# Low parts of the streamed weight tiles on DVE in one step of 1024 columns, instead of on POOL in four

## The chip, the cores and the metric

The kernel runs on one core of a Trainium2 chip. The metric is the device time of one execution in microseconds; lower is better. A measurement is the median of several runs. The engines are named as the profile names them: PE (matmul) with its weight loads PEld, DVE (vector), ACT (scalar), POOL (GpSimd) and SP, whose queue issues most transfers.

## The reference, cut to what matters

The model is a two-layer diffusion backbone of width 1024 over 512 latent tokens and 256 context tokens, in float32. Each layer does, in essence:

```python
h  = rms_norm(x,  pre_g[i]) * (1.0 + scale)  + shift     # 512 x 1024
hc = rms_norm(xc, pre_g[i]) * (1.0 + cscale) + cshift    # 256 x 1024
p  = t @ w_in                # for t = h and hc: q, k, v, z
y  = (attention(q, k, v) * silu(z)) @ w_out
x  = x + gate * rms_norm(y, post_g[i])
```

Layer 0 is a differential attention with 8 heads (two softmaxes per head, one subtracted from the other), with outputs for latent and context tokens. Layer 1 is a grouped-query attention with 8 query heads and 2 key/value heads, with outputs for the latent tokens alone. `w_in` has 4096 columns in layer 0 and 2560 in layer 1.

## The kernel before, in words

**Products from split operands.** To keep float32 accuracy, each operand is split into a high part (a rounded cast, `whi` for weights) and a low part (what the cast left over, `wlo`). A product is three matmuls, in `mm3` (lines 146 to 149): high by high (L147), one operand's low part by the other's high part (L148), and high by low (L149). Weights come in tiles of 128 x 1024.

**The stream of weights.** `WStream` (`ws`) keeps a list of tiles in the order in which they are needed. For each it calls `wsplit` (lines 206 to 212): SP issues the load into a `raw` tile (L208; 512 KB), ACT casts it into `whi` (L210), and the engine named in the list subtracts `whi` from `raw` to make `wlo`, in `pieces` (L204). `pieces` cuts the columns into steps of 256 where that engine is POOL, and does them in one step where it is DVE:

```python
n = w // -(-w // 256) if eng is nc.gpsimd else w
for i in range(0, w, n):
    eng.tensor_tensor(dst[:, i:i + n], a[:, i:i + n], b[:, i:i + n], op)
```

There are two `raw` buffers, so a load starts when the tile two before it has been read by both ACT and the engine of the low part. There are three or four pairs of `whi`/`wlo`; a pair comes free when PE has used it.

Of the streamed tiles, 28 are layer 0's q, k, v and z, 20 are layer 1's (of which 8 to 11 are its k and v), and 16 are the two `w_out`. The first four tiles of layer 0 go another way, in quarters, through `w_split`. Before the change the low parts of 46 of the 64 streamed tiles are made by POOL (44 that the change touches, and tiles 9 and 11 of layer 1, which `KVE` gives to it), and those of 18 by DVE (the 16 of `w_out`, and tiles 8 and 10).

**What else the engines do.** In attention, `s_units` (layer 0, from line 829) and `s1_units` (layer 1) make scores on PE; DVE takes the maximum (L850, L1384), ACT the exponential `p` (L853, L1390), DVE the reciprocal of its sum (L856, L1391), POOL scales `p` (L218), and in layer 0 DVE then adds the two softmaxes (L861). PE transposes `p` (L910, L1405), ACT and DVE split the result into `ah` (L913, L1408) and `al` (L914, L1409), and PE multiplies by the values (L154). For layer 1's queries, `q_proj` takes a projection out of PSUM with DVE (`ta` L1243, `tb` L1245), POOL adds the two (`q`, L1248) and makes the factor `qrs` (L1256, L1257); `q_tr` transposes `q` on PE (L1341) and splits it into `qh` (ACT, L1344) and `ql` (DVE, L1345). At the start of layer 1, DVE also makes the residual gate from streamed tiles `gw` (L1443, L1445).

**What sets the order.** The program is written out in the order that a planner in the kernel (`flow`, with a running clock, costs and due times) chooses; it doesn't look at the engine that makes a low part. The framework then puts the instructions of each engine in order, by priorities and by its own estimate of times. On the chip each engine works through its list in that order; an instruction that waits holds all behind it on that engine.

Of the kernel before, what the change touches and what calls it, by code (L numbers as in the profile page):

```python
# [82 lines left out]
def tile_backbone(  # L83
# [23 lines left out]
    nc = tc.nc  # L107
# [155 lines left out]
    ws = WStream()  # L263
# [3 lines left out]
    def add_wout(layer):  # L267
        for c, n in (OUTC, OUTC1)[layer]:
            per = 1024 // n
            for k in range(KT // per):  # L270
                src = w_out[layer, k * per * P:(k + 1) * per * P, c:c + n].rearrange("(k p) n -> p k n", p=P)
                ws.add(("o", layer, c, k), src, nc.vector)
# [9 lines left out]
    for kind, h in fill0:  # L282
        a_keys += {"qk": [(h, 0), (h, 1)], "v": [(h, 2), (h + 1, 2)], "z": [(h, 3)]}[kind]
    for h, i in a_keys:
        ws.add((h, i), a_w[h * 4 + i], nc.gpsimd)
    add_wout(0)
    for i in (8, 9, 10, 11):
        ws.add(i, b_w[i], (nc.vector, nc.gpsimd)[KVE[i - 8]])
    for kind, i in [("q", 0)] + fill1:
        for g in (2 * i, 2 * i + 1) if kind == "q" else (12 + i,):  # L290
            ws.add(g, b_w[g], nc.gpsimd)
    add_wout(1)

    def after(prev):
# [1359 lines left out]
```

## Time and profile before

| | us |
|---|---|
| median of three runs (826.65, 828.59, 830.71) | 828.59 |
| the profiled execution, as timed | 825.61 |
| its span in the profile | 823.8 |

The page of the profile gives each engine's busy time as a share of the span. The view by line groups equal instructions: how many, their busy time, the mean of one, and how long the engine was idle just before them and which instruction ended that. The view of waits sums that idle time by who waited for whom. The view of windows gives each engine's busy time and the granted PE clock in a stretch of time. The timeline lists instructions by start and duration, with the idle time before one and its releaser in brackets.

### The profile page before, as it was taken

The page shows a single profiled execution, that of the slowest core. Times are in us where ns is not written, and L with a number is a line of the kernel's source. Part 1 is how long each engine was busy: PE and PEld are TensorE (multiplying, and loading weights), DVE is VectorE, ACT ScalarE, POOL GpSimd, SP SyncE. Part 2 cuts the span into 40 slices and gives each one's busy share as a digit, 9 for nine tenths or more (in the row PEclk, how much of TensorE's full clock was granted, in tenths as well). Part 3 has the DMA queues.
Part 4 walks back from the last instruction along what each step waited for, and adds up shares of the span by engine and source line. Part 5 has one row for each costly group of instructions (what it writes and reads, how often), then busy time and mean ns, then how long its engine had stood idle before and what let it go on. Part 6 is the DMA issues. An engine that isn't in the chain of part 4 may idle for free. (4 is left out here: it accounts for less than half of the span.)

```text
span 823.8 us, 14331 instructions
## 1 busy us (share of the span) xinstructions
PE 792.1 (96%) x5436; PEld 699.6 (85%) x5436; DVE 483.3 (59%) x897; ACT 452.6 (55%) x985; POOL 439.3 (53%) x612
## 2 busy tenths in 40 slices
PE   7999998999999999999999999999989999999997
PEld 4688897898878898878988898898978899988986
DVE  3745566664858425765277843664676666665534
ACT  5424457565575634764467742664336665676631
POOL 1134847965476853875733212576878854643101
PEclk9999999999999999999999999999999999999999
DMA  9924201122124321414310051031641310111102
GB/s 343 355 78 141 87 29 58 63 86 78 65 103 128 115 78 65 167 34 152 122 53 26 27 205 52 13 123 52 194 140 52 103 52 2 53 52 52 47 31 102
DMA packets 35236, 77.76 MB, mean 94 GB/s; under 512 B 3424, under 2 KB 10336, under 8 KB 35168
## 3 DMA queue, kind: packets, MB, share of 16 engines
q1 hardware_dynamic: 31600, 71.71, 25.5%
q10 hardware_dynamic: 3568, 5.16, 1.8%
q8 instruction: 42, 0.69, 0.3%
q14 instruction: 26, 0.21, 0.1%
HBM read 70.56 MB, written 2.10 MB: 88 GB/s over the span
## 5 line engine op out<-in xcount | busy, mean ns | idle before, releaser
L204 POOL TENSOR_TENSOR wlo<-raw,whi 128x256 fp32r<-128x256 f32 x196 | 149.7, 795 | 104.9 <-ACT whi L210 68.6
L147 PE MATMUL bk<-whi,h 128*128 128x256 f32 (+1 forms) x592 | 177.5, 302 | 5.9 <-DVE tb L1245 2.0
L148 PE MATMUL bk<-wlo,h 128*128 128x256 f32 (+1 forms) x592 | 176.2, 299 | 0.3 <-DVE wlo L204 0.3
L149 PE MATMUL bk<-whi,h 128*128 128x256 f32 (+1 forms) x592 | 175.1, 299 | 0.1
L147 PE MATMUL bk<-h,whi 128*128 128x512 f32 (+2 forms) x416 | 147.0, 354 | 3.2 <-ACT sq L942 1.5
L149 PE MATMUL bk<-h,wlo 128*128 128x512 f32 (+2 forms) x416 | 144.9, 349 | 0.0
L148 PE MATMUL bk<-h,whi 128*128 128x512 f32 (+2 forms) x416 | 144.6, 348 | 0.0
L147 PEld LDWEIGHTS bk<-whi,h 128*128 128x128 f32 x592 | 112.9, 191 | 15.5 <-issue 3.6
L148 PEld LDWEIGHTS bk<-wlo,h 128*128 128x128 f32 x592 | 113.1, 191 | 4.0 <-DVE wlo L204 0.5
L149 PEld LDWEIGHTS bk<-whi,h 128*128 128x128 f32 x592 | 112.3, 191 | 3.9 <-DVE h L1209 0.3
L218 POOL TENSOR_SCALAR p<-p,sm 128x768 f32<-128x768 f32 (+1 forms) x80 | 68.4, 858 | 65.8 <-DVE sm L1391 30.0
L210 ACT CAST whi<-raw 128x1024 fp32r<-128x1024 f32 x64 | 67.3, 1052 | 48.3 <-PE bk L148 19.2
L147 PEld LDWEIGHTS bk<-h,whi 128*128 128x128 f32 x416 | 78.2, 188 | 17.4 <-issue 5.1
L149 PEld LDWEIGHTS bk<-h,wlo 128*128 128x128 f32 x416 | 78.1, 188 | 8.4 <-issue 1.3
L148 PEld LDWEIGHTS bk<-h,whi 128*128 128x128 f32 x416 | 78.3, 188 | 6.8 <-issue 0.3
L853 ACT ACTIVATE p<-sc,sm 128x768 f32<-128x768 f32 (+1 forms) x68 | 59.6, 879 | 30.1 <-DVE sm L850 30.0
L850 DVE TENSOR_REDUCE sm<-sc 128x1 f32<-128x768 f32 (+1 forms) x68 | 60.5, 916 | 16.5 <-PE sc L845 16.5
L204 POOL TENSOR_TENSOR sz<-sz,za 128x192 f32<-128x192 f32 (+1 forms) x48 | 32.5, 699 | 42.0 <-ACT za L184 42.0
L861 DVE SCALAR_TENSOR_TENSOR p<-p,sm,p 128x768 f32<-128x768 f32 (+1 forms) x34 | 39.0, 1146 | 24.4 <-POOL p L218 23.5
L913 ACT CAST ah<-bk 128x512 fp32r<-128x512 f32 x56 | 31.8, 589 | 30.8 <-PE bk L910 26.8
L914 DVE TENSOR_TENSOR al<-bk,ah 128x512 fp32r<-128x512 f32 x56 | 37.4, 683 | 16.9 <-ACT ah L913 16.8
L1409 DVE TENSOR_TENSOR al<-bk,ah 128x512 fp32r<-128x512 f32 x48 | 32.1, 685 | 25.6 <-ACT ah L1408 24.8
(236 smaller groups left out, 1688.4 us busy)
## 6 DMA issues: line engine op xcount, KB each, us to landing
raw<-in_a_w SPq DMA_DIRECT2D x28, 512.0 KB, 3.5
araw<-in_ada_w SPq DMA_DIRECT2D x12, 1024.0 KB, 5.2
raw<-in_b_w SPq DMA_DIRECT2D x20, 512.0 KB, 3.9
ag<-in_ada SPq DMA_DIRECT2D x16, 512.0 KB, 7.8
raw<-in_w_out SPq DMA_DIRECT2D x16, 512.0 KB, 3.5
sw<-qr ACTq DMA_DIRECT2D x32, 128.0 KB, 2.1
gw<-in_ada_w SPq DMA_DIRECT2D x8, 512.0 KB, 4.1
xnt<-in_xlT SPq DMA_DIRECT2D x4, 512.0 KB, 5.7
```

The costliest lines, as they stand in the source:

```text
L147: nc.tensor.matmul(o, ahi, bhi, start=start, stop=False)
L148: nc.tensor.matmul(o, ahi, blo, start=False, stop=False)
L149: nc.tensor.matmul(o, alo, bhi, start=False, stop=stop)
L204: eng.tensor_tensor(dst[:, i:i + n], a[:, i:i + n], b[:, i:i + n], op)
L210: nc.scalar.copy(hi, r)
L218: (nc.vector if eng == "v" else nc.gpsimd).tensor_scalar(dst, src, s_, 1.0, ALU.mult, ALU.mult)
L850: nc.vector.tensor_reduce(mx, scv, AX.XY if nk == T else AX.X, ALU.max, negate=True)
L853: nc.scalar.activation(pv_, scv, AF.Exp, bias=mx, accum_out=l[:, m:m + 1])
L861: nc.vector.scalar_tensor_tensor(ps_[0], pt, r, ps_[0], ALU.mult, ALU.add)
L913: nc.scalar.copy(ah, tr)
L914: nc.vector.tensor_tensor(al, tr, f32(ah), ALU.subtract)
L1409: nc.vector.tensor_tensor(al, tr, f32(ah), ALU.subtract)
```

## The change

The list of weight tiles names DVE instead of POOL for all of layer 0's tiles (`a_keys`) and for layer 1's q and z. So `pieces` makes one step of 128 x 1024 of each on DVE instead of four of 128 x 256 on POOL.

```diff
     for h, i in a_keys:
-        ws.add((h, i), a_w[h * 4 + i], nc.gpsimd)
+        ws.add((h, i), a_w[h * 4 + i], nc.vector)
     add_wout(0)
     for i in (8, 9, 10, 11):
         ws.add(i, b_w[i], (nc.vector, nc.gpsimd)[KVE[i - 8]])
     for kind, i in [("q", 0)] + fill1:
         for g in (2 * i, 2 * i + 1) if kind == "q" else (12 + i,):
-            ws.add(g, b_w[g], nc.gpsimd)
+            ws.add(g, b_w[g], nc.vector)
```

The order changes with it on every engine, since the framework orders by its estimates. Two places matter below. In the names, the first number tells tiles of one kind apart.

The first is POOL at the start of layer 1's attention, while the queries of heads 0 and 1 are made. Before, from the third of four sums, `q_849`, to the third weight tile:

```order
L1248 TENSOR_TENSOR q_849_6541<-ta_850_6542,tb_851_6543 128x256
L204 TENSOR_TENSOR wlo_861_6591<-raw_859_6588,whi_860_6590 128x256 x4
L204 TENSOR_TENSOR wlo_864_6600<-raw_862_6597,whi_863_6599 128x256 x3
L1256 TENSOR_SCALAR qrs_855_6577<-sm_852_6572 128x2
L204 TENSOR_TENSOR wlo_864_6600<-raw_862_6597,whi_863_6599 128x256
L1248 TENSOR_TENSOR q_856_6581<-ta_857_6582,tb_858_6583 128x256
L1257 TENSOR_TENSOR qrs_855_6577<-qrs_855_6577,mhalf_85 128x2
L204 TENSOR_TENSOR wlo_879_6681<-raw_877_6678,whi_878_6680 128x256 x4
```

After, the same stretch of POOL:

```order
L1248 TENSOR_TENSOR q_849_6445<-ta_850_6446,tb_851_6447 128x256
L1256 TENSOR_SCALAR qrs_855_6481<-sm_852_6476 128x2
L1257 TENSOR_TENSOR qrs_855_6481<-qrs_855_6481,mhalf_85 128x2
L1248 TENSOR_TENSOR q_856_6485<-ta_857_6486,tb_858_6487 128x256
L1256 TENSOR_SCALAR qrs_885_6621<-sm_882_6616 128x2
```

Eight pieces of two weight tiles have left the list ahead of `q_856`, the last of the four sums that PE transposes, and four behind it. DVE there, after the change, from the first new weight step to `ql_874`:

```order
L204 TENSOR_TENSOR wlo_861_6495<-raw_859_6492,whi_860_6494 128x1024
L1445 SCALAR_TENSOR_TENSOR gate1_5212<-gw_868_6516,scol_107,gate1_5212 128x512
L204 TENSOR_TENSOR wlo_864_6501<-raw_862_6498,whi_863_6500 128x1024
L1243 TENSOR_TENSOR ta_857_6486<-bk0_68,ropeb_5841 128x256
L1245 TENSOR_TENSOR tb_858_6487<-bk0_68,ropeb_5841 128x2x64 x2
L1445 SCALAR_TENSOR_TENSOR gate1_5212<-gw_868_6516,scol_107,gate1_5212 128x512
L1443 TENSOR_SCALAR gate1_5212<-gw_869_6520,scol_107 128x512
L1326 TENSOR_SCALAR qrs_855_6481<-qrs_855_6481 128x2
L1445 SCALAR_TENSOR_TENSOR gate1_5212<-gw_869_6520,scol_107,gate1_5212 128x512
L204 TENSOR_TENSOR wlo_879_6579<-raw_877_6576,whi_878_6578 128x1024
L1445 SCALAR_TENSOR_TENSOR gate1_5212<-gw_870_6524,scol_107,gate1_5212 128x512
L1345 TENSOR_TENSOR ql_874_6553<-bk3_71,qh_873_6552 128x512
```

Before, the same stretch of DVE ended like this:

```order
L1445 SCALAR_TENSOR_TENSOR gate1_5296<-gw_870_6626,scol_107,gate1_5296 128x512
L1445 SCALAR_TENSOR_TENSOR gate1_5296<-gw_871_6630,scol_107,gate1_5296 128x512
L183 SCALAR_TENSOR_TENSOR za_881_6689<-sz_880_6687,za_881_6689 128x512
L1243 TENSOR_TENSOR ta_887_6731<-bk0_68,ropeb_5925 128x256
L1245 TENSOR_TENSOR tb_888_6732<-bk0_68,ropeb_5925 128x2x64 x2
L1445 SCALAR_TENSOR_TENSOR gate1_5296<-gw_871_6630,scol_107,gate1_5296 128x512
L1345 TENSOR_TENSOR ql_874_6655<-bk3_71,qh_873_6654 128x512
```

DVE has got three steps of 1024 columns, and `ql_874` has moved ahead of the gate's last steps and of the fifth query tile.

The second place is POOL in layer 0, head 0. Before, `wlo_178` stood in front of the gate product `sz` and of the softmax `p_182`:

```order
L218 TENSOR_SCALAR p_172_1367<-p_172_1367,sm_170_1352 128x768
L204 TENSOR_TENSOR wlo_178_1402<-raw_176_1399,whi_177_1401 128x256 x4
L204 TENSOR_TENSOR sz_158_1247<-sz_158_1247,za_169_1332 128x192 x2
L218 TENSOR_SCALAR p_182_1442<-p_182_1442,sm_180_1427 128x768
L204 TENSOR_TENSOR gT_98_810<-gT_98_810,sz_158_1247 128x256
```

After:

```order
L218 TENSOR_SCALAR p_172_1346<-p_172_1346,sm_170_1331 128x768
L204 TENSOR_TENSOR sz_158_1226<-sz_158_1226,za_169_1311 128x192 x2
L204 TENSOR_TENSOR gT_98_798<-gT_98_798,sz_158_1226 128x256
L204 TENSOR_TENSOR sz_158_1226<-sz_158_1226,za_175_1370 128x192 x2
L218 TENSOR_SCALAR p_182_1418<-p_182_1418,sm_180_1403 128x768
```

The four pieces are gone, and `p_182` has another gate product in front of it. On DVE `wlo_178` now stands between `za_169` and the step L945 on `gT_98`.

## Prediction

> **What bounds the kernel now.** I read the page first.
>
> ```profile
> span 823.8 us, 14331 instructions
> PE 792.1 (96%) x5436; PEld 699.6 (85%) x5436; DVE 483.3 (59%) x897; ACT 452.6 (55%) x985; POOL 439.3 (53%) x612
> ```
>
> PE is busy for 792.1 of 823.8 us, so 31.7 us is all that a change on another engine can win, unless PE itself becomes faster, and nothing here touches its instructions. The next question is where the 31.7 us lie. I cut the span where the stages change and asked for windows; columns are the stretch, then busy time of PE, PEld, DVE, ACT and POOL, the granted PE clock and the transfers.
>
> ```profile
> 0.00:41.00 41.00, 35.36 (x216) 24.21 (x217) 21.69 (x56) 21.05 (x38) 7.01 (x14) 0.96 0.95 351
> 41.00:577.00 536.00, 523.79 (x3647) 458.29 (x3646) 314.48 (x556) 296.87 (x649) 303.11 (x414) 1.00 0.25 85
> 577.00:618.00 41.00, 37.04 (x263) 35.20 (x262) 28.42 (x50) 16.47 (x44) 33.05 (x42) 0.96 0.51 167
> 618.00:803.00 185.00, 181.03 (x1206) 167.82 (x1205) 109.70 (x221) 114.90 (x245) 92.31 (x130) 1.00 0.15 49
> 803.00:824.00 21.00, 14.91 (x111) 14.12 (x110) 9.00 (x16) 3.27 (x12) 3.81 (x12) 0.95 0.28 100
> ```
>
> PE idles 5.6 us at the start and 6.1 at the end, where no tile that the change touches is split. What is left is 12.2 us in 41 to 577, 4.0 in 577 to 618 and 4.0 in 618 to 803: some 20 us. The third row stands out: POOL is busy there for 33.05 of 41 us, more than in any other row, and PE loses a tenth of its time. Who holds PE up is in the view of waits (us in total, times, longest).
>
> ```profile
> PE bk L147 <- DVE tb L1245: 2.0, 1, 2.0
> PE bk L910 <- DVE al L914: 1.8, 2, 1.6
> ...
> PE sc L147 <- ACT qh L1344: 1.5, 1, 1.5
> ...
> PE bk L910 <- DVE p L861: 1.1, 1, 1.1
> ...
> PE bk L1341 <- POOL q L1248: 0.4, 1, 0.4
> ...
> PE bk L148 <- DVE wlo L204: 0.3, 1, 0.3
> ...
> PE bk L1405 <- DVE ql L1345: 0.2, 1, 0.2
> ```
>
> No row here names a low part made by POOL: PE never waits for those directly. Behind the start, DVE ends 15 of these waits, from 2.0 us for `tb` to 0.2 for `ql`, 12.0 us together, and ACT most of the rest. The change works on the engine that ends most waits, and only through what stands before or behind the moved steps.
>
> **What is removed and added.** The view by line, with shapes kept apart:
>
> ```profile
> L204 POOL TENSOR_TENSOR wlo<-raw,whi 128x256 fp32r<-128x256 f32 x196 | 149.7, 795 | 104.9 <-ACT whi L210 68.6 <-ACT whi L530 36.0
> ...
> L861 DVE SCALAR_TENSOR_TENSOR p<-p,sm,p 128x768 f32<-128x768 f32 x32 | 37.0, 1158 | 24.3 <-POOL p L218 23.5
> ...
> L204 DVE TENSOR_TENSOR wlo<-raw,whi 128x1024 fp32r<-128x1024 f32 x18 | 22.3, 1240 | 16.0 <-ACT whi L210 16.0
> ...
> L1445 DVE SCALAR_TENSOR_TENSOR gate<-gw,scol,gate 128x512 f32<-128x512 f32 x14 | 15.3, 1096 | 3.9 <-DMA gw<-in_ada_w 3.7
> ```
>
> POOL loses 44 x 4 = 176 of its 196 pieces: 176 x 0.795 = 139.9 us, which leaves it 299 us. DVE gets 44 steps of the kind that it already has 18 of: 44 x 1.240 = 54.6 us, 483.3 becomes 538 (65% of the span). A tile's low part takes 1.24 us in place of 4 x 0.795 = 3.2. Neither engine gets near PE's 792, so the loads decide nothing; the places do. Loads keep their number and size, and a `raw` buffer comes back some 2 us sooner where DVE is prompt.
>
> **Term A, the start of layer 1's attention (577 to 618).** On POOL the pieces of two tiles stand ahead of the last query sum `q_856`:
>
> ```profile
> 590.25 6.71 POOL L204 TENSOR_TENSOR wlo<-raw,whi 128x256 fp32r<-128x256 f32 x7
> ...
> 597.38 1.25 POOL L204 TENSOR_TENSOR wlo<-raw,whi 128x256 fp32r<-128x256 f32 x1
> 598.60 0.72 POOL L1248 TENSOR_TENSOR q<-ta,tb 128x256 f32<-128x256 f32 x1
> ```
>
> PE waits three times in this stretch, and these make up all of its 3.96 idle us there (41 - 37.04):
>
> ```profile
> 599.38 0.44 PE L1341 MATMUL bk<-ident,q 128*128 128x128 f32 x2 [0.44 <-POOL q L1248]
> 603.37 0.44 PE L147 MATMUL sc<-kh,qh 128*128 128x384 f32 x1 [1.53 <-ACT qh L1344]
> 606.32 0.39 PE L147 MATMUL bk<-whi,h 128*128 128x256 f32 x1 [1.99 <-DVE tb L1245]
> ```
>
> The first wait is POOL's doing. The second has the same root, by way of a buffer: the load of the next weight tile goes out as soon as POOL has done the first four of the seven pieces (590.25 + 4 / 7 x 6.71 = 594.1), and ACT holds `qh` behind the cast of that tile.
>
> ```profile
> 594.45 0.34 SPq L208 DMA_DIRECT2D raw<-in_b_w  x1
> ...
> 599.56 1.05 ACT L210 CAST whi<-raw 128x1024 fp32r<-128x1024 f32 x1 [3.71 <-DMA raw<-in_b_w]
> ...
> 602.73 0.58 ACT L1344 CAST qh<-bk 128x512 fp32r<-128x512 f32 x1
> ```
>
> In the new order (first place above) `q_856` has no piece in front of it, and `wlo_861` is one step on DVE. The third wait goes as well: `ql` and the transposes come forward, and the fifth query tile, whose bank PE waited for, falls back. So 0.44 + 1.53 + 1.99 = 3.96 us go. What is late next is `ql_874`: the step `wlo_879` and a gate step now stand ahead of it, and that gate step waits for its transfer.
>
> ```profile
> 600.87 1.10 DVE L1445 SCALAR_TENSOR_TENSOR gate<-gw,scol,gate 128x512 f32<-128x512 f32 x1 [2.83 <-DMA gw<-in_ada_w]
> ...
> 606.19 0.73 DVE L1445 SCALAR_TENSOR_TENSOR gate<-gw,scol,gate 128x512 f32<-128x512 f32 x1
> ```
>
> PE stood ready at 603.37 - 1.53 = 601.84, or 601.4 without the first wait; `ql` can't end before 600.87 + 1.10 + 0.68 (the length of such a split, as in the last DVE row quoted below) = 602.65. That is a wait of 1.2 us, between 0 (PE has four matmuls to do first) and 2.4 (if `wlo_879` comes behind the transfer, too). The three new steps themselves, 3.7 us, find 12.6 us in which DVE idles in this window (41 - 28.42), 2.83 of them right before 600.87. A = -3.96 + 1.2 = **-2.8**.
>
> The gate step takes 1.10 us beside POOL's pieces and 0.73 at 606.19; the mean of 14 is 1.096. [...]
>
> **Term B, head 0 of layer 0.** Here POOL's pieces delay a softmax:
>
> ```profile
> 135.25 3.54 POOL L204 TENSOR_TENSOR wlo<-raw,whi 128x256 fp32r<-128x256 f32 x4 [3.02 <-ACT whi L210]
> ...
> 140.21 0.91 POOL L218 TENSOR_SCALAR p<-p,sm 128x768 f32<-128x768 f32 x1
> ```
>
> ```profile
> 138.29 0.15 DVE L856 RECIPROCAL sm<-sm 128x1 f32<-128x1 f32 x1
> ...
> 141.15 1.48 DVE L861 SCALAR_TENSOR_TENSOR p<-p,sm,p 128x768 f32<-128x768 f32 x1 [0.90 <-POOL p L218]
> ```
>
> ```profile
> 142.69 0.33 PE L910 MATMUL bk<-ident,p 128*128 128x128 f32 x1 [1.11 <-DVE p L861]
> ```
>
> Its factor was there at 138.44, POOL came to it at 140.21, 1.8 us late; DVE stood for 0.90 and PE for 1.11. Without the pieces (second place above) that goes, though another gate product now stands ahead of `p_182`. B = **-1.1**, or 0 if that product is as late. Elsewhere POOL ends 23.5 us of DVE's waits at L861, but PE stands behind no other of them, so I count nothing more.
>
> **Term C, the new steps on DVE.** Each waits for ACT's cast and holds what is queued behind it: maxima, `al`, `tb`, which PE needs. No row shows the 44, but 18 like them are there. They waited 16.0 us for `whi`, and PE paid twice: the 0.3 above and this, near 757 us.
>
> ```profile
> 755.96 1.22 DVE L204 TENSOR_TENSOR wlo<-raw,whi 128x1024 fp32r<-128x1024 f32 x1 [2.15 <-ACT whi L210]
> ...
> 757.97 0.68 DVE L1409 TENSOR_TENSOR al<-bk,ah 128x512 fp32r<-128x512 f32 x1
> ```
>
> ```profile
> 758.70 0.50 PE L147 MATMUL bk<-h,whi 128*128 128x512 f32 x1 [0.55 <-DVE al L1409]
> ```
>
> DVE stood 2.15 us for a cast, `al` came behind the step and a maximum, PE idled 0.55. So 18 steps cost PE 0.85 us and 44 cost 44 / 18 x 0.85 = **+2.1**. The bounds are 0 and the 9.3 of the rival below; I take the 18, since they are the same instruction in the same queue.
>
> **The sum.** -2.8 - 1.1 + 2.1 = -1.8. The profiled execution took 825.61 us and would take 823.8. It lay 3.0 us under the median of the runs, 828.59; the same step from that median gives **826.8 us**, -0.2%. No change up to 0.5% (4.1 us) can be told here from none, as the three runs lie 4.06 us apart.
>
> **Rivals.** *DVE's queue becomes the brake (slower).* DVE ends 15 of PE's waits. If half of them get one more step of 1.24 us in front, PE pays 15 / 2 x 1.24 = 9.3 us: 837.9, +1.1%. The likeliest place is near 642, where ACT's new order puts the cast of `raw_991` ahead of the exponential that stood before it:
>
> ```profile
> 642.14 0.98 ACT L1390 ACTIVATE p<-sc,sm,qrs 128x768 f32<-128x768 f32 x1
> ...
> 646.05 1.05 ACT L210 CAST whi<-raw 128x1024 fp32r<-128x1024 f32 x1 [2.58 <-DMA raw<-in_b_w]
> ```
>
> That softmax then starts some 5 us later. It decides from about 8 us of new waits, 6 or 7 steps that reach PE whole, since A and B give back 3.9. For it: 65% load on an engine that works in order. Against it: 16.0 us of such waiting cost PE 0.85 so far. [...]
>
> *POOL was the brake (faster).* If the new steps find DVE idle everywhere, C is 0 and A is the full 3.96; the granted clock, 0.96 in that stretch, would rise to 1.00, as in the rows where PE hardly stops: 41 x 0.04 = 1.6 us. With B that is -6.7: 821.9, -0.8%. For it: 140 us less on POOL, 23.5 us of DVE's waits on it. Against: only 0.4 us of PE's waits name POOL.
>
> *Nothing moves.* PE's 792.1 us are untouched and slack absorbs the rest: 828.6. That the steps are not moved at all is excluded by the order.
>
> **Chances and range.** Forecast 0.36 and nothing moves 0.10, both within 0.5%: 0.46. POOL was the brake, 0.26, over 0.5% faster. DVE's queue, 0.28, over 0.5% slower. The range takes in both rivals, each with half the spread of the runs (2.0 us): 821.9 - 1.9 = 820.0 and 837.9 + 2.0 = 839.9. My forecast's own range is 824 to 830.
>
> **What would show it.** Right: DVE near 535 us and POOL near 300; the waits at `q` L1248 and `tb` L1245 gone, PE idle in the new 577 to 618 at 1 to 2 us, with `ql` as releaser; PE waits behind `wlo` L204 or rows right after it at about 3 us. Wrong: DVE rows held by `whi` L210 for far more than 16.0 x 62 / 18 = 55 us and PE idle above 36 us (the queue), or below 27 (POOL). PE's busy time off 792 by more than 2 us would mean that the new PE order matters in itself, which I have priced at nothing.

## The result and the profile after

The changed kernel takes 825.9 us (median of 18 runs) beside 827.62 us for the kernel before (median of 18 on the same chip): ratio 0.9974, 95% interval 0.9963 to 0.9984. That is 1.7 us less in the medians and 2.2 by the ratio. It lies within the half per cent that the prediction's three runs could not tell from none; with 18 runs the interval is clear of 1. One of the 18 executions took 1537.28 us, at a granted clock of 1.0; its cause is open, and the ratio leaves it out. The profiled execution took 825.35 us (before: 825.61), with a span of 823.6 us (before: 823.8).

The page of the profile after:

```profile
span 823.6 us, 14197 instructions
...
PE 794.6 (96%) x5436; PEld 698.8 (85%) x5436; DVE 522.8 (63%) x941; ACT 451.5 (55%) x985; POOL 319.0 (39%) x436
```

POOL has lost 120 us and DVE has gained 39.5. PE's own busy time, which nothing was meant to touch, has grown by 2.5 us. The windows at the same cuts as before:

```profile
41.00:577.00 536.00, 524.02 (x3625) 455.73 (x3624) 344.00 (x583) 296.01 (x647) 221.87 (x294) 1.00 0.25 84
577.00:618.00 41.00, 39.37 (x295) 37.87 (x294) 34.08 (x62) 18.96 (x51) 18.88 (x23) 1.00 0.53 170
618.00:803.00 185.00, 180.74 (x1196) 166.57 (x1195) 113.66 (x226) 111.98 (x238) 67.33 (x93) 1.00 0.15 49
```

In 577 to 618 PE idles 1.63 us instead of 3.96, and its granted clock is 1.00 instead of 0.96. In 41 to 577 the idle time is nearly what it was, 11.98 us after 12.21. By these two rows the idle time alone should have won 2.6 us (2.33 + 0.23). Who PE waits for, in the view of waits:

```profile
PE sc L147 <- ACT p L1390: 4.1, 5, 1.6
PE bk L910 <- DVE al L914: 3.3, 4, 1.8
...
PE sc L147 <- ACT qh L1344: 1.0, 1, 1.0
PE bk L379 <- POOL sqs L377: 0.9, 1, 0.9
...
PE bk L147 <- ACT qr L732: 0.5, 1, 0.5
...
PE bk L148 <- DVE wlo L204: 0.3, 1, 0.3
...
PE bk L149 <- DVE wlo L204: 0.3, 1, 0.3
```

The rows for `q` L1248, `tb` L1245, `p` L861 and one of `p` L853 are gone. New or longer are those for `al`, `sqs`, `qr` and layer 1's exponential `p`. Before, two rows for the exponentials of layers 0 and 1 were:

```profile
PE sc L845 <- ACT p L853: 1.4, 1, 1.4
PE bk L147 <- ACT p L1390: 1.2, 1, 1.2
```

A window at fixed times doesn't tell how far the work has got. For that I use landmarks: the same work of PE in both traces. The view by tile of `p` gives, for the transposes of layer 0 (first row) and of layer 1 (second row), the count, the durations, and when the first and the last started. Before:

```profile
L910 PE MATMUL bk<-ident,p x224: 270/272/330, 89.8 to 470.4; 128*128 128x128 f32 x112
L1405 PE MATMUL bk<-ident,p x192: 270/272/329, 619.0 to 776.1; 128*128 128x128 f32 x192
```

After:

```profile
L910 PE MATMUL bk<-ident,p x224: 270/272/332, 92.3 to 473.6; 128*128 128x128 f32 x112
L1405 PE MATMUL bk<-ident,p x192: 270/272/328, 615.8 to 775.8; 128*128 128x128 f32 x192
```

Layer 0's attention ends 3.2 us later than before (473.6 against 470.4), and layer 1's 0.3 us earlier. So the small result is a difference of two larger ones: layer 0 lost what layer 1 won. With the last matmul on the tile `ag` as the start (50.2 us before, 49.8 after), "layer 0" below is the time from there to the last transpose of layer 0, and "layer 1" the time from that to the last transpose of layer 1: 420.2 and 305.7 us before, 423.8 and 302.2 after, +3.6 and -3.5. The windows cut at the landmarks of layer 0, before and after, hold as many instructions of PE (2874 each):

```profile
50.20:470.40 420.20, 411.22 (x2874) 356.60 (x2867) 255.52 (x444) 242.53 (x504) 253.07 (x326) 1.00 0.25 84
49.80:473.60 423.80, 414.39 (x2874) 356.82 (x2867) 283.93 (x472) 242.37 (x504) 176.94 (x214) 1.00 0.25 83
```

PE's idle time in layer 0 goes from 8.98 to 9.41 us only; 3.2 of the 3.6 us are busy time. These are single executions: that of before lies 2.0 us under its median, that of after 0.55, so the landmarks can be off by a microsecond or two.

### The profile page after: what moved, and what is told of

The parts are those of the page before. It is cut to its first block, busy times and chain, and to the rows that moved or that the text cites. A ratio compares the mean times of both kernels' runs of the same rounds, so it can differ in the third digit from the quotient of the medians.

```text
span 823.6 us, 14197 instructions
## 1 busy us (share of the span) xinstructions
PE 794.6 (96%) x5436; PEld 698.8 (85%) x5436; DVE 522.8 (63%) x941; ACT 451.5 (55%) x985; POOL 319.0 (39%) x436
## 5 line engine op out<-in xcount | busy, mean ns | idle before, releaser
L204 DVE TENSOR_TENSOR wlo<-raw,whi 128x1024 fp32r<-128x1024 f32 (+2 forms) x65 | 81.3, 1250 | 42.8 <-ACT whi L210 39.2
L853 ACT ACTIVATE p<-sc,sm 128x768 f32<-128x768 f32 (+1 forms) x68 | 59.6, 879 | 42.3 <-DVE sm L850 42.0
L850 DVE TENSOR_REDUCE sm<-sc 128x1 f32<-128x768 f32 (+1 forms) x68 | 60.7, 917 | 17.9 <-PE sc L845 17.9
L204 POOL TENSOR_TENSOR qr<-qr,rope 128x256 f32<-128x256 f32 x28 | 27.8, 1014 | 78.7 <-DMA sw<-qr 78.0
L1409 DVE TENSOR_TENSOR al<-bk,ah 128x512 fp32r<-128x512 f32 x48 | 32.1, 685 | 23.9 <-ACT ah L1408 23.0
L845 PE MATMUL sc<-qk,qk 64*128 64x384 f32 (+1 forms) x396 | 46.5, 356 | 0.2 <-POOL qk L204 0.2
L861 DVE SCALAR_TENSOR_TENSOR p<-p,sm,p 128x768 f32<-128x768 f32 (+1 forms) x34 | 39.0, 1148 | 10.7 <-POOL p L218 8.9
```

Source lines behind the costliest of these rows:

```text
L845: prev = nc.tensor.matmul(sc[m][:, j if nk == T else m, :w], a[r, tok], b[r, c], start=i == 0, stop=i == 2)
L850: nc.vector.tensor_reduce(mx, scv, AX.XY if nk == T else AX.X, ALU.max, negate=True)
L853: nc.scalar.activation(pv_, scv, AF.Exp, bias=mx, accum_out=l[:, m:m + 1])
L861: nc.vector.scalar_tensor_tensor(ps_[0], pt, r, ps_[0], ALU.mult, ALU.add)
L1409: nc.vector.tensor_tensor(al, tr, f32(ah), ALU.subtract)
```

## The experiments

My theory after the result: the two layers are two separate effects. Layer 1 wins because POOL's list is freed around 590 us (term A). Layer 0 loses either because DVE's new steps hold up what is queued behind them (term C, too small in the prediction), or because PE's matmuls now stand in another order, since the framework orders by its own estimates. The rivals for each run are in its expectation. Ratios are against runs of the kernel before on the same chip. "Half" counts the stretches of some 3.4 us in which PE's granted clock was 0.50, in layer 0 and layer 1; the last section shows one, and each costs PE up to 1.7 us (half of 3.4). In the row with three `raw` buffers layer 0 holds 2885 instructions of PE instead of 2874, so its 421.9 us aren't quite the same work.

| kernel | ratio to before (95%) | layer 0 | layer 1 | half |
|---|---|---|---|---|
| before | 1 | 420.2 | 305.7 | 0, 1 |
| after | 0.9974 (0.9963 to 0.9984) | 423.8 | 302.2 | 0, 0 |
| layer 0 alone on DVE | 1.0021 (1.0008 to 1.0034) | 423.6 | 305.3 | 1, 1 |
| layer 1 alone on DVE | 0.9943 (0.9930 to 0.9956) | 420.7 | 301.7 | 1, 0 |
| four tiles of layer 1 on DVE | 0.9958 (0.9944 to 0.9972) | 420.5 | 303.8 | 0, 1 |
| the other twelve of layer 1 | 0.9938 (0.9920 to 0.9956) | 420.5 | 303.5 | 1, 2 |
| after, in four steps | 0.9958 (0.9944 to 0.9972) | 424.5 | 299.6 | 1, 0 |
| before, POOL in one step | 1.0027 (1.0013 to 1.0042) | 424.9 | 306.3 | 2, 2 |
| before, three `raw` buffers | 0.9974 (0.9959 to 0.9988) | 421.9 | 303.0 | 0, 1 |
| no low parts | 0.9947 (0.9927 to 0.9967) | 427.1 | 297.7 | 1, 0 |
| DVE, before's order in layer 0 | 0.9941 (0.9921 to 0.9962) | 422.0 | 302.1 | 1, 0 |
| POOL, after's order | 1.0034 (1.0019 to 1.0049) | 425.8 | 305.6 | 1, 0 |
| DVE, before's order | 1.0012 (0.9999 to 1.0025) | 420.6 | 310.7 | 1, 3 |
| 20 + 16 tiles on DVE, before's order in layer 0 | 0.9911 (0.9884 to 0.9938) | 417.7 | 301.6 | 0, 0 |

**Layer 0 alone.** The list of layer 1's q and z names POOL again:

```diff
-            ws.add(g, b_w[g], nc.vector)
+            ws.add(g, b_w[g], nc.gpsimd)
```

> Only the 28 tiles of layer 0 go to DVE; layer 1's 16 stay on POOL. Theory (the two layers cancel): the trace of the kernel after reached 757 us 0.3 us earlier than the trace before, but 557 us 3.4 us later, so layer 0 alone costs +2 to +3.5 us (+0.3 to +0.4%), with DVE near 510 us busy, POOL near 355, and the waits at `q` L1248 and `tb` L1245 back in the stretch 577 to 618 as in before. Rival 1 (the shift inside layer 0 is only a drift of one profiled execution): within 1 us of before. Rival 2 (the prediction's terms): B -1.1 and C 28/18 x 0.85 = +1.3, so +0.2 us.

Measured: 829.79 us beside 828.09, ratio 1.0021, so slower by 1.7 us in the medians and 3.4 us in the landmarks of layer 0. That is more than rival 2's +0.2, and it is no drift of one execution.

**Layer 1 alone.** The same edit the other way round, in the list of layer 0:

```diff
-        ws.add((h, i), a_w[h * 4 + i], nc.vector)
+        ws.add((h, i), a_w[h * 4 + i], nc.gpsimd)
```

> Only layer 1's 16 tiles (queries and z) go to DVE; layer 0 stays on POOL. Theory (the two layers cancel): the gain between 557 and 757 us comes alone, -3 to -4.5 us (-0.4 to -0.5%), faster than both kernels; PE idles about 2 us in 577 to 618 in place of 4.0, with no wait at `q` L1248. Rival 1 (one profile's drift): within 1 us of before. Rival 2 (the prediction's terms): A -2.8 and C 16/18 x 0.85 = +0.8, so -2.0 us.

Measured: 823.54 us, ratio 0.9943, 4.7 us faster; layer 1 takes 4.0 us less. The two halves add up: +1.7 and -4.7 make -3.0, and the whole change, whose interval reaches from -3.1 to -1.3, made -2.2. Half of the change is better than the whole.

**Four tiles of layer 1.**

```diff
-            ws.add(g, b_w[g], nc.gpsimd)
+            ws.add(g, b_w[g], nc.vector if kind == "q" and i in (1, 2) else nc.gpsimd)
```

> Only the four tiles of layer 1's query pairs 1 and 2 (keys 2 to 5) go to DVE; these are the ones that POOL splits between about 580 and 600 us. Theory (term A sits at this place and nowhere else in layer 1): nearly the whole gain of layer 1 comes with these four, -2.5 to -4 us, PE idle in 577 to 618 at 2 us or less. Rival (the gain of layer 1 is spread over all its tiles, or is made by PE's order behind 618 us): -0.5 to -1.5 us, a quarter of that of the 16.

**The other twelve.**

```diff
-            ws.add(g, b_w[g], nc.gpsimd)
+            ws.add(g, b_w[g], nc.gpsimd if kind == "q" and i in (1, 2) else nc.vector)
```

> Layer 1's other 12 tiles (queries of pairs 0 and 3, and z) go to DVE; the four of pairs 1 and 2 and all of layer 0 stay on POOL. The complement of the run with the four tiles. Theory (term A sits in the four tiles alone): within 1.5 us of before, the waits at `q` L1248, `qh` L1344 and `tb` L1245 all still there. Rival (the gain is spread over layer 1): -1 to -3.5 us.

The two belong together. The four tiles gave 0.9958, 3.5 us, as my theory had it. Then the twelve should have given next to nothing, and they gave 0.9938, 5.1 us: more than the four, and as much as all sixteen. So the gain isn't the sum of what the tiles do, and "term A sits in these four" has fallen. With the twelve, `q` is gone from PE's waits though POOL still cuts the four, `qh` still costs 1.8 us and `ql` appears with 1.0. It seems that several rearrangements of the same 40 us win about as much; which property they share is open.

**DVE in four steps.** The 44 tiles on DVE, but cut as POOL cuts them (`four` is true for these tiles alone):

```diff
-        pieces(eng, lo, r, f32(hi), ALU.subtract)
+        for j in range(0, 1024, 256) if eng is nc.vector and four else (0,):
+            n = 256 if eng is nc.vector and four else 1024
+            pieces(eng, lo[:, j:j + n], r[:, j:j + n], f32(hi)[:, j:j + n], ALU.subtract)
```

> As the kernel after, but DVE makes the low parts of the 44 tiles in four steps of 256 columns instead of one of 1024. The work moved is the same and only the cutting differs. Theory (the one step counts little: what matters is which engine does it): within 2 us of after; DVE's busy time grows by 44 x (4 x about 0.35 - 1.25) = about 7 us. Rival 1 (long steps in DVE's queue are what layer 0 pays for): 1 to 3.5 us faster than after. Rival 2 (DVE's load is what layer 0 pays for): 1 to 3 us slower than after.

Measured: 824.79 us, ratio 0.9958. After's own ratio of 0.9974 has an interval that overlaps with this one, so the cutting isn't told apart; it didn't cost anything, although four steps take 4 x 0.494 = 1.98 us instead of 1.29 and DVE's busy time rises to 539.4, by 16.6 us where I had expected 7, from an estimate of 0.35 us a step. Layer 0 gets no shorter (424.5, one half-speed stretch included), which gives no sign that the length of a step is what it pays for. PE's order differs from after's from the start, which leaves this run inconclusive on the rest.

**POOL in one step.**

```diff
-        pieces(eng, lo, r, f32(hi), ALU.subtract)
+        eng.tensor_tensor(lo, r, f32(hi), ALU.subtract)
```

> As before, all low parts that POOL made stay on POOL, but in one step of 1024 columns instead of four of 256. Theory (what gains is that POOL's list is freed of the work, not the number of steps): within 2 us of before or slower, since a step of about 3.2 us holds `q` and `p` on POOL at least as long as four of 0.8; the wait at `q` L1248 stays or grows. Rival (the four pieces themselves are the cost, one POOL step of 1024 takes well under 3.2 us): 2 to 4 us faster than before. In layer 0 this run also tells how far the end of the stage moves when only the framework's order changes and no work changes its engine: over 1.5 us either way would mean that order alone can make layer 0's loss.

Measured: 830.38 us, ratio 1.0027, slower as the theory said, although one step of 1024 takes POOL 2.42 us where four took 3.18. The wait for `q`, which was to stay or grow, is gone; those for `tb` (2.9 us) and `qh` (1.2) stay. Layer 0 is 4.7 us longer with no work on another engine. Two half-speed stretches may make 3.4 us of that, so it is no more than a hint that order can do this.

**Three `raw` buffers.** The buffers of `raw` go from two to three at every place that has them, and the scratch `jk` of layer 1 goes to bfloat16:

```diff
-        r = wp.tile([P, 1024], F32, tag="raw", name=nm("raw"), bufs=2)
+        r = wp.tile([P, 1024], F32, tag="raw", name=nm("raw"), bufs=3)
...
-                jk = t1p.tile([P, P], F32, tag="jk", name=nm("jk"), bufs=1)
+                jk = t1p.tile([P, P], BF, tag="jk", name=nm("jk"), bufs=1)
```

> As before, with three `raw` buffers instead of two (and a scratch tile of layer 1's squares in bfloat16 to make room, whose values are not used). The next load then need not wait for POOL's pieces. Theory (the 1.53 us at `qh` come by way of the buffer): the wait of PE at `qh` L1344 in 577 to 618 goes, those at `q` (0.44) and `tb` (2.0) stay, and the whole is 1 to 2.5 us faster than before. Rival (the buffer is not what held it; POOL's list is): within 1 us of before, `qh` late as before.

Measured: 826.01 us, ratio 0.9974, 2.2 us faster. The wait for `qh` is gone, as the theory of the buffer had it. It isn't shown to be the buffer's doing, since PE's order is another here, too. Against the theory `tb` falls to 0.5 us, and `q` now costs 1.4 and `ql` 1.8: the next waits took part of the place.

**No low parts.** For the 44 tiles neither engine makes a low part, and PE reads the high part instead, in as many matmuls:

```diff
+        if eng is None:
+            return hi, hi
         pieces(eng, lo, r, f32(hi), ALU.subtract)
```

> The low parts of the 44 tiles are left out on both engines (PE reads the high part in their place, with as many matmuls as before), so neither POOL nor DVE has the work. This is the most that moving it can win. Theory (DVE's new steps cost layer 0 its 3.4 us, by the waits behind them): layer 0 gets 1 to 3 us faster than before, layer 1 at least 4 us, in all -5 to -7 us against before and 3 to 5 us faster than the kernel after. Rival (layer 0's loss is PE's new order, which the framework chooses as soon as the pieces leave POOL): layer 0 ends 1 to 4 us later than before here too, and the whole is only 1 to 3 us faster than before.

The view by tile of `p`:

```profile
L912 PE MATMUL bk<-ident,p x224: 270/273/475, 92.4 to 476.9; 128*128 128x128 f32 x112
L1407 PE MATMUL bk<-ident,p x192: 270/272/312, 616.4 to 774.6; 128*128 128x128 f32 x192
```

Even with the work gone from both engines, layer 0 ends at 476.9 us: 6.5 us later than before, and 3.3 later than with DVE doing it. One half-speed stretch is included (up to 1.7 us). No new step in DVE's queue can explain that. Layer 1 gets 8.0 us shorter. In all 823.55 us, ratio 0.9947: a little short of the theory's 5 to 7 us and beyond the rival's 1 to 3. For layer 0 the rival was right in direction, and its 1 to 4 us were too few.

**The order held.** To part engine and order, the next kernels write down in which order PE's 5294 matmuls stood in one kernel and hold another to it (5294 are the calls in the program; the profile counts 5436 instructions of PE). All of PE's matmuls are recorded as they are traced (`pes`), and edges that force no wait, only the order of issue, are laid between neighbours. The other engines' lists are not held; the framework orders them around PE's:

```diff
+    order = [pes[i].ins for i in array.array('H', zlib.decompress(base64.b64decode(PE_ORDER)))]
+    for a, b in zip(order, order[1:]):
+        tc.add_manual_dep(b, a.name, dep, reason='order')
```

In their traces all matmuls carry the line of a helper (L198 or L236) and all transposes that of another (L202 or L240); other lines are later by 91 or 129. The first holds the kernel after to before's order up to 565 us:

> The kernel after (all 44 tiles on DVE), but PE's matmuls up to about 565 us are held in the order that they have in the kernel before; behind that the order is that of after. Theory (layer 0 lost its 3.4 to 3.8 us because the framework put PE's list into another order, not because DVE has the steps): layer 0 ends within 1.5 us of before, or earlier, since terms B and the wait at `p` L853 may still go; the whole is 4 to 6 us faster than before. Rival (DVE's steps cost it, term C): layer 0 stays 2 to 4 us longer than before, the whole within 1.5 us of after.

The second is the kernel before, held to after's order:

> The kernel before (POOL makes the low parts, in four steps), with PE's matmuls held from start to end in the order that they have in the kernel after. Theory (order makes layer 0's loss; freeing POOL makes layer 1's gain): layer 0 2 to 4 us longer than before, and layer 1 loses its gain: `q` comes late again in 577 to 618, so the whole is 2 to 6 us slower than before. Rival for layer 1 (its gain too is PE's order): layer 1 is 2 to 4 us shorter than before, the whole within 1.5 us of after. Rival for layer 0 (DVE's steps make the loss): layer 0 within 1 us of before.

The third is the kernel after, held to before's order:

> The kernel after (DVE makes the low parts, in one step), with PE's matmuls held from start to end in the order that they have in the kernel before. Layer 0 is as in the run with only layer 0's order held, so it shows how far that repeats. Layer 1: theory (term A: POOL freed, PE no longer waits for `q` and `qh`, but for `tb` it still does, since the fifth query tile keeps its early place): 1.5 to 3 us shorter than before. Rival (the gain is the order): within 1 us of before in layer 1.

The view by tile of `p`, of the kernel before held to after's order:

```profile
L240 PE MATMUL bk<-ident,p x224: 270/272/333, 93.5 to 477.2; 128*128 128x128 f32 x112
L240 PE MATMUL bk<-ident,p x192: 270/272/328, 622.3 to 782.8; 128*128 128x128 f32 x192
```

And of the kernel after held to before's order:

```profile
L240 PE MATMUL bk<-ident,p x224: 270/272/330, 89.8 to 470.4; 128*128 128x128 f32 x112
L240 PE MATMUL bk<-ident,p x192: 270/272/329, 615.3 to 781.1; 128*128 128x128 f32 x192
```

Layer 0, first rows: with POOL doing the work as ever, after's order alone costs it 5.6 us (425.8 against 420.2; the start lies 1.2 us later, at 51.4). One half-speed stretch is included, and 3.8 us are two waits for `sqs`, which POOL makes, where after has 0.9. With DVE doing the work in before's order it takes 420.6, one half-speed stretch included. So the order makes layer 0's loss and the engine doesn't; what in the order makes PE's busy time longer is open. Holding layer 0's order alone gave 822.12 us, ratio 0.9941, 4.9 us faster, as the theory said. The profiled execution, at 825.18 us, was one of its three longer ones; the other four took 821.4 to 822.1. Its layer 0 took 422.0 us, 1.8 less than after, but 1.8 more than before, a little over what I had allowed. The third kernel has the same order and the same engine there and took 420.6, so two executions differ by 1.4 us. Most of the 1.8 us went at one place near 345 us, where PE stood 2.55 us in two waits, with a half-speed stretch behind them:

```profile
345.27 1.06 PE L198 MATMUL bk<-araw,s 128*32 128x512 f32 x8 [1.73 <-DVE al L1005]
...
347.16 1.20 PE L198 MATMUL sc<-qk,qk 64*128 64x256 f32 x12 [0.82 <-ACT p L944]
```

A cleaner comparison lies in the traces. By the names (without buffer numbers) and shapes of its matmuls, PE's order is the same from start to end in the kernel with layer 0's order held, in the one with layer 1 alone on DVE, and in the last one below. They differ in the engine for layer 0's 28 tiles. With POOL for all the ratio is 0.9943, with DVE for all 0.9941: in that order moving layer 0's tiles neither wins nor loses.

Layer 1, second rows: here both of my theories failed. After's order without DVE wins nothing (305.6 against 305.7). DVE without after's order loses 5.0 us (310.7; two more half-speed stretches may make 3.4 of it), where I expected a gain of 1.5 to 3. Only both together win 3.5, of which before's one half-speed stretch may make 1.7. The waits behind 577 us show how; with POOL in after's order:

```profile
PE bk L240 <- POOL q L1377: 1.8, 1, 1.8
PE bk L236 <- DVE tb L1374: 1.8, 2, 1.0
...
PE bk L240 <- POOL qrs L1386: 1.0, 1, 1.0
```

With DVE in before's order:

```profile
PE bk L236 <- DVE tb L1374: 4.1, 2, 2.5
PE bk L240 <- DVE al L1538: 2.2, 1, 2.2
PE sc L236 <- ACT p L1519: 1.9, 1, 1.9
```

`q` comes late where POOL still cuts weights, in the order that counts on it early. `tb` comes late where DVE now cuts weights, in the order that wants it early. Each order fits the engine for which it was made.

**Put together.** Layer 1's sixteen tiles and the first twenty of layer 0's on DVE, the last eight on POOL, PE's list in before's order up to 565 us:

```diff
-    for h, i in a_keys:
-        ws.add((h, i), a_w[h * 4 + i], nc.vector)
+    for j, (h, i) in enumerate(a_keys):
+        ws.add((h, i), a_w[h * 4 + i], nc.vector if j < 20 else nc.gpsimd)
```

> A version put together from the runs so far: layer 1's 16 tiles and the first 20 of layer 0's 28 on DVE, the last 8 of layer 0 on POOL, PE's matmuls up to about 565 us held in the order of before, behind that the order chosen freely. Theory (in before's order DVE's steps win terms B and the wait at `p` L853 up to 340 us, 0.8 to 2.3 us, and it is the last 8 tiles that cost PE waits at about 345 us, 1.2 in one run and 4 in the other): 5.5 to 6.5 us faster than before, a little faster than the run with layer 1's 16 alone, and no wait of PE near 345 us. Rival (the wait near 345 us comes whichever engine splits there, or layer 0 gains nothing): 3.5 to 5 us faster, no better than layer 1's 16 alone.

```profile
L202 PE MATMUL bk<-ident,p x224: 270/272/330, 89.9 to 467.6; 128*128 128x128 f32 x112
L202 PE MATMUL bk<-ident,p x192: 270/272/328, 609.2 to 769.2; 128*128 128x128 f32 x192
```

Measured: 819.32 us beside 828.02, ratio 0.9911 (0.9884 to 0.9938), 7.4 us faster by the ratio and the best of all, though its interval still overlaps with that of layer 1 alone (0.9930 to 0.9956). The wait near 345 us is gone, and layer 1 is 4.1 us shorter. Layer 0 is 2.5 us shorter than before. Of that, 1.7 us are waits: 1.11 for `p` L861, 0.27 for `al` right behind it and 0.64 for `gT` near 154 us are gone, and 0.30 for `wlo` near 67 us is new. The 1.40 us for `p` L853, which the theory counted on, stay (L944 here):

```profile
126.11 1.32 PE L198 MATMUL sc<-qk,qk 64*128 64x384 f32 x12 [1.39 <-ACT p L944]
```

## Why the prediction came out as it did

The time was right: 1.8 us forecast, 1.7 measured in the medians. The reasons were right only in part, and that the number fits is partly luck. By the prediction's terms layer 0 was to cost 0.2 us and layer 1 to win 2.0; moved alone they cost 1.7 and won 4.7. The two errors, 1.5 and 2.7 us, point opposite ways.

**What failed: "Priced at nothing", PE's order.** I wrote that nothing touches PE's instructions, and that its busy time off 792 by more than 2 us would mean that the order matters in itself. It came out at 794.6. The order cost layer 0 some 3.6 us here (5.6 with POOL doing the work, a half-speed stretch included), and most of it doesn't show as waits: between the landmarks PE idles 9.41 us after 8.98, while the same work takes 414.39 us of busy time after 411.22.

**Term A, -2.8: right place and waits, too small, and then partly given back.** `q`, `qh` there and `tb` went, and the idle time fell by 2.3 us in the fixed window. By the landmarks, from the last transpose of layer 0 to the first of layer 1 it is 142.2 us after 148.6, with 7.19 us of idling before and 4.20 after. Part of it is the clock, 0.96 to 1.00, which I had left to a rival at 1.6 us. From the first to the last transpose of layer 1 it is 160.0 us after 157.1, but PE idles only 0.3 us longer there (4.26 after 3.97): 13 instructions of PE (1060 after 1047) have moved into this stretch from the one before. So of the 2.9 us a part is moved work and only a part is given back; the net, over the same work, is -3.5.

The releaser that I named was wrong. `ql` was no hindrance; the wait of 1.63 us came some 9 us later, for the first exponential, whose scale on DVE started 1.0 us after the reduction had ended and took 1.23:

```profile
608.45 0.94 DVE L1384 TENSOR_REDUCE sm<-sc 128x1 f32<-128x768 f32 x1
...
610.38 1.23 DVE L1387 TENSOR_TENSOR sm<-sm,qrs 128x1 f32<-128x1 f32 x1
...
611.70 0.99 ACT L1390 ACTIVATE p<-sc,sm,qrs 128x768 f32<-128x768 f32 x1 [1.84 <-DVE sm L1387]
...
612.84 0.45 PE L147 MATMUL sc<-kh,qh 128*128 128x384 f32 x1 [1.63 <-ACT p L1390]
```

And the mechanism is not POOL alone: the gain needs the new order as well, and other sets of tiles reach it too.

**Term B, -1.1: right in kind, seen only with the order held.** The wait went, and one of 1.40 us for `p` L853 with it. In the order that the framework chose, `al`, `qr` and `sqs` took their place. With before's order the wait of 1.11 us goes with 0.27 for `al` and 0.64 for `gT` close behind it, but the 1.40 us for `p` L853 stay; layer 0 gains 2.5 us in all there.

**Term C, +2.1: not found.** The 62 steps wait 39.2 us for `whi` (I had bounded the forecast at 55), but PE's waits that name `wlo` are 0.3 twice, one of them there before, and twenty of layer 0's steps in before's order cost 0.30 us that can be seen (the wait near 67 us). The waits near 345 us with all 28 on DVE are the one place where they may have cost; DVE also stood 3.21 us for the transfer of `sw` until 341.82 us in the kernel with layer 0's order held (0.44 until 340.74 before), and I didn't part the two. The 0.85 us per 18 steps came from two places, and two places make no rate.

**The rivals.** DVE's queue didn't become the brake: PE idles 29.0 us (823.6 - 794.6), less than the 31.7 before. "POOL was the brake" was right on its clock and waits, and layer 1 alone came near its 0.8% (0.9943). (The lower end of the range, with the 2.0 us that it names, is 819.9 and not 820.0.)

**Loads.** DVE came to 522.8, not the 538 of the sum. Its 62 steps took 1.286 us each where I had 1.240, but its other work got 17.9 us shorter (483.3 + 79.7 - 22.3 - 522.8). POOL came to 319.0, not 299. The 139.9 us that I took off were too much: pieces in a row overlap in the profile, so 196 with a mean of 0.795 us were busy for 149.7 and not 155.8. And its other work grew by 13.8 us (303.4 after 289.6, without the pieces).

## What to carry to other kernels

Where a framework orders the instructions by its estimates, a change of engine is two changes, and the order can be the larger: hold the order of the engine that bounds the kernel, and measure both apart. Compare traces at landmarks of the same work, not in windows of fixed times, and look at stages one by one, since a result near zero may be two effects. A tile's engine is then chosen stage by stage: here 36 of the 44 moves, with before's order in layer 0, gave the best median, and all 44 with a new order were worth less than a third of that (0.26% of 0.89%).

## What the runs showed of the hardware

**A granted clock of 0.50 for 3.4 us after a wait of 1.82 us, not always.** Here are the two places behind the same wait of 1.82 us for `al` near 430 us. With layer 0 alone on DVE:

```profile
429.28 1.12 PE L910 MATMUL bk<-ident,p 128*128 128x128 f32 x4 [1.82 <-DVE al L914]
```

After:

```profile
431.06 0.66 PE L910 MATMUL bk<-ident,p 128*128 128x128 f32 x4 [1.82 <-DVE al L914]
```

The same four transposes take 1.12 us in one and 0.66 in the other. The windows of a microsecond show the granted clock (the number behind POOL's column), with layer 0 alone on DVE:

```profile
429.00:430.00 1.00, 0.72 (x4) 0.73 (x5) 0.95 (x7) 0.90 (x3) 0.01 (x1) 0.55 0.00 0
430.00:431.00 1.00, 1.00 (x6) 1.00 (x5) 0.87 (x2) 0.57 (x1) 0.90 (x1) 0.50 0.00 0
431.00:432.00 1.00, 1.00 (x7) 1.00 (x6) 0.95 (x2) 0.02 (x1) 0.00 (x0) 0.50 0.00 0
432.00:433.00 1.00, 1.00 (x7) 0.87 (x8) 0.67 (x1) 0.00 (x0) 0.00 (x0) 0.75 0.00 0
433.00:434.00 1.00, 1.00 (x13) 0.75 (x11) 0.00 (x0) 0.00 (x0) 0.00 (x0) 1.00 0.06 16
```

The sum of what is missing to 1.00 is 0.45 + 0.5 + 0.5 + 0.25 = 1.7 us, so at 0.50 it lasted 3.4 us. After, the windows 428 to 431 and 431 to 435 show 1.00. By such windows the fourteen kernels of the table have 19 stretches in layer 0 and layer 1: 17 lack 1.69 to 1.71 us, and two lack 3.41, each counted as two. The kernel before has one such stretch between 606 and 611 us, behind its waits for `qh` and `tb`: that was the 0.96 of its window. It differs from run to run, too: the granted clock of the whole span averages 0.9922 over 19 runs of before and 0.9961 over 17 of after. How long PE idles doesn't settle it: from 41 to 803 us POOL in after's order idles 23.2 us, and its whole span averages 0.9946 over 12 runs; three `raw` buffers idle 16.0 us there and average 0.9900 over 12. What starts such a stretch isn't shown: a wait of 1.82 us had one behind it once and once not.

**The gate step on DVE takes 0.99 to 1.10 us where POOL cuts weights beside it, and 0.77 to 0.83 where it doesn't.** The step L1445, mean in ns of 14: 1096 before, 1090 with layer 0 alone moved, 989 with POOL in after's order; 772 after, 771 with layer 1 alone moved, 780 with no low parts at all, 827 with DVE in before's order. So it goes with whether POOL cuts weights beside it. What lengthens the step isn't shown. Term A counted on 1.10 us; after's 0.772 is nearer the 0.73 of the prediction's row at 606.19.
